# Where the operands of TensorE's matmuls lie in SBUF: one offset modulo 512 bytes for all weight buffers, another for the projections' inputs

## The chip, the cores and the metric

The kernel runs on one core of one Trainium2 chip, in one launch. The metric is the device time of one execution in microseconds (us), and lower is better. Times before come from three timed executions and from one execution that the hardware profiler recorded.

## The reference, cut to what matters

Two residual layers over 256 tokens of width 1024, all in float32. Layer 0 mixes tokens with a Griffin block (input projections, a short convolution, gates, a linear recurrence, an output projection), layer 1 with RWKV-7 time mixing. Behind each mixer stands a PEER channel mixer, which picks 16 of 16384 experts for each token and head:

```python
for i in range(DEPTH):                      # 2 layers
    m = rglru_mixer(x, ...) if i % 2 == 0 else rwkv7_time_mix(x, ...)
    x = layer_norm(ALPHA * x + m, ...)
    # PEER: scores -> top 16 of 128 x 128 -> gate = softmax(scores)
    #   act = gelu(x . u[eid]);  c = sum over the chosen (gate * act) * v[eid]
    c = peer_channel_mix(x, peer_w_q[i], peer_sub_keys[i], peer_u[i], peer_v[i])
    x = layer_norm(ALPHA * x + c, ...)
```

## The kernel before

The kernel does not gather the chosen experts. It multiplies x by all 16384 rows of u, multiplies the result by a dense matrix of gates that is zero where an expert was not chosen, and multiplies that by all rows of v. A PEER layer therefore streams 16 blocks of query weights (the first 2 of them take another path), 128 blocks of u and 128 blocks of v, each 128 x 1024 float32 (512 KB), through one class, `Stream`. The Griffin and RWKV projections go the same way.

For each block, `Stream.prep` makes two parts: `whi`, the block rounded to float32r by ScalarE (line 90), and `wlo`, the remainder, by VectorE (line 91). There are three pairs of buffers, whi0/wlo0 to whi2/wlo2, taken in turn. A product of two float32 matrices is three float32r matmuls: high by high, high by low, low by high.

Each matmul has two SBUF operands. The stationary one (128 x 128) is brought in by a weight load that runs under the matmul before it; the moving one (128 x 256 or 128 x 512) is streamed. The two big groups of matmuls differ in which operand is which:

```python
# proj (line 317), for u, the query weights, and the Griffin and RWKV inputs: weights stationary, x moving, 256 columns
for db in range(NDB):                               # 8, so 24 matmuls in a call
    s = slice(db * 128 + c0, db * 128 + c0 + n)
    for l, r in ((wh, hi), (wh, lo), (wl, hi)):
        nc.tensor.matmul(out, l[:, s], r[:, db, :], start=(k == 0), stop=(k == 23))
# rows (line 327), for v and the output projections: coefficients stationary, weights moving, 512 columns
for k, (l, r) in enumerate(((ch, wh), (ch, wl), (cl, wh))):
    for dh in dhs:                                  # 12 matmuls in a call: 2 x 3 x 2
        nc.tensor.matmul(accs[2 * tb + dh], l[:, ts], r[:, dh * 512:dh * 512 + 512], ...)
```

Slices of an operand lie a multiple of 512 bytes apart, so an operand keeps its offset modulo 512 through a whole call. These offsets, read from the built program's allocation, are:

```
tile (bytes modulo 512)                        before            after
whi0, wlo0                                     192, 192          192, 192
whi1, wlo1                                     384, 448          192, 192
whi2, wlo2                                     64, 64            192, 192
xhi, xlo: input of u, query weights, Griffin   128               128
ch, cl: coefficients of v                      128               192
xh, xl: input of Griffin's gates (line 530)    64                128
mr, mk, mv: inputs of RWKV's r, k, v           288               128
yh, yl: stationary in Griffin's output         64                192
oh, ol: stationary in RWKV's output            384               224
sl: late coefficients and weights of v         352               352
```

Below, d is the offset of the next stationary slice minus that of the operand that streams meanwhile, modulo 512. In proj of u, before, d is 64 with buffer 0, 256 and 320 with whi1 and wlo1, and 448 with buffer 2. In rows of v it is 448, 256 and 192, and 64. At the end of a PEER layer, the last four blocks of v and their coefficients both lie in the tile `sl`, where d is 0.

While proj of u runs, VectorE and ScalarE do what `_peer_side` yields between calls: the choice of the top 16 and the dense gates. How much of it stands between two calls is set by written budgets in the order of the code, not by the clock. VectorE's `wlo` of a block stands in that same queue, and the third matmul of a call waits for it.

Of the kernel before, what the change touches and what calls it, by code (L numbers as in the profile page):

```python
# [8 lines left out]
F32 = mybir.dt.float32  # L9
F32R = mybir.dt.float32r  # L10
F16 = mybir.dt.float16
# [8 lines left out]
T = 256  # L20
NDB = 8
# [15 lines left out]
class Stream:  # L37
# [1 line left out]


    RAW, SPLIT = 4, 3
    OFF = (0, 0, 192, 64, 128, 0, 64)

    def __init__(self, nc, pool):
        self.nc, self.pool = nc, pool
        self.items, self.nd, self.np, self.nu = [], 0, 0, 0
        self.raw, self.parts, self.held, self.live = {}, {}, [], 0
        self.place, self.marks = {}, set()
        self.nr = 0

    def room(self):


        for n in range(self.RAW):
            self.pool.tile([128, 1024], F32, name="wraw", bufs=self.RAW)
        for n, off in enumerate(self.OFF):
            if off:
# [74 lines left out]
class Sched:  # L132
# [15 lines left out]
    def seq(self, items, bias):  # L148

        self.lists.append(list(items))
        self.bias.append(bias)
# [64 lines left out]
class Trunk:  # L218
    def __init__(self, ctx, tc, a):
        self.ctx, self.tc, self.nc, self.a = ctx, tc, tc.nc, a  # L220
        nc = self.nc
        self.const = ctx.enter_context(tc.tile_pool(name="const", bufs=1))
        self.stage = ctx.enter_context(tc.tile_pool(name="stage", bufs=1))
        self.keep = ctx.enter_context(tc.tile_pool(name="keep", bufs=1))
        self.ps = ctx.enter_context(tc.tile_pool(name="ps", bufs=1, space=PSUM))
        self.ws = Stream(nc, self.stage)
        self.ws.room()


    def acc(self):  # L230
# [240 lines left out]
    def rglru(self, li, last=False, parts=True):  # L471
        nc = self.nc
        with self.tc.tile_pool(name="rg", bufs=1) as pool:
            col = self.rgcol
            accs = [self.acc() for _ in range(4)]
            tm = pool.tile([128, 5, NM], F32, name="rgtm")
# [89 lines left out]
            y, late = {}, []  # L566
# [2 lines left out]
                nc.vector.scalar_tensor_tensor(gb[:, m], gb[:, m], 1.0 / ALPHA, tt[:, m], op0=ALU.mult, op1=ALU.mult)  # L569

            def yh(m):
                y[m] = pool.tile([128, T], F32R, name="yh", bufs=self.LATE), pool.tile([128, T], F32R, name="yl", bufs=self.LATE)
                nc.scalar.activation(y[m][0], gb[:, m], AF.Copy)

# [3 lines left out]
            def out(m):  # L578
# [26 lines left out]
                xhi=seq(xhi, lambda m: [("xc", m)], "xhi", None, one("act", .36), 0),  # L605
                xlo=seq(xlo, lambda m: [("xhi", m)], "xlo", None, one("dve", .34), 0),
# [25 lines left out]
    def rwkv(self, li, x, last=False, parts=True):  # L632
# [9 lines left out]
        pool = ctx.enter_context(self.tc.tile_pool(name="rw", bufs=1))  # L642
# [2 lines left out]
        mp = ph1.enter_context(self.tc.tile_pool(name="rwm", bufs=1))  # L645
        cp = None
        col = self.rwcol
        one_ = pool.tile([128, 8], F32, name="one")
        W0, A0, KK, KA, RK, LG, LB = 6, 7, 8, 9, 10, 11, 12
        r, av = ([pool.tile([128, 4, T], F32, name=f"{nm}{n}") for n in range(2)] for nm in "ra")  # L650
# [534 lines left out]
    def peer(self, l, li, x, last=False, parts=True):  # L1185
# [3 lines left out]
        keys, p = None, None  # L1189
        for what, tb, dh, f in x:  # L1190
# [5 lines left out]
            if p is None:  # L1196
                self.ws.fill()
                keys, *ws = (self.ws.get(False) for _ in range(3))
                p = self.mm()
# [9 lines left out]
        with self.tc.tile_pool(name="peer", bufs=1) as pool:  # L1209
# [8 lines left out]
            def fill(us):  # L1218
                self.budget += us
                while self.budget > 0:  # L1220
                    c = next(side, None)
                    if c is None or c < 0:
                        self.budget = 0.0
                        return
                    self.budget -= c

            def finish():
                while self.g_done < T:
                    assert next(side, 0) >= 0 or self.g_done == T
# [4 lines left out]
            def scores(q):  # L1234
                for tb in range(2):
                    sp = self.aux()
                    for a in range(2):
                        nc.tensor.matmul(sp[:, a * 128:a * 128 + 128], qt[q][:, a, tb * 128:tb * 128 + 128],  # L1238
                                         keys[:, ((q - 1 + a) % 8) * 128:((q - 1 + a) % 8) * 128 + 128], start=True, stop=True)
                    nc.scalar.activation(self.sc[tb][:, q - 1:q + 1, :], sp[:, :256].rearrange("p (a n) -> p a n", a=2), AF.Copy)  # L1240
                self.q_done = q + 1

            for q in range(16):
# [3 lines left out]
                if q >= 2:  # L1247
                    if q % 2 == 0:
                        p = self.mm()
# [9 lines left out]
            def act(sp, i):  # L1259


                n, pv, sv = self.g_done, sp.rearrange("p (a t) -> p a t", a=2), two(i)
                if n < T:
                    nc.scalar.activation(sv[:, :, n:], pv[:, :, n:], AF.Gelu_apprx_tanh)  # L1264
                if n:
                    nc.scalar.activation(pv[:, :, :n], pv[:, :, :n], AF.Gelu_apprx_tanh)
                    nc.vector.tensor_tensor(sv[:, :, :n], pv[:, :, :n], sv[:, :, :n], op=ALU.mult)
                self.s_done = i + 2


            for i in range(128):
                if i % 2 == 0:
                    prev, sp = (sp if i else None), self.mm()
                self.proj(sp[:, (i % 2) * T:(i % 2) * T + T])
                if i == 0:
                    scores(15)
                    self.ws.done()
                assert self.chosen or i < 80
                if i % 2 == 0 and i:
                    act(prev, i - 2)  # L1280
                if i == 127:
                    act(sp, 126)
                fill(SFILL)
                if i == 124:
                    finish()

                    first = [pool.tile([128, T], F32R, name=f"c{n}") for n in range(2)]
                    nc.scalar.activation(first[0], S[0][:, 0, :], AF.Copy)
                    nc.vector.tensor_tensor(first[1], S[0][:, 0, :], first[0].bitcast(F32), op=ALU.subtract)

            ch = self.keep.tile([128, 4, 2, T], F32R, name="ch", tag="xhi")
            cl = self.keep.tile([128, 4, 2, T], F32R, name="cl", tag="xlo")

            def c_at(i):

                if i < 128 - self.LATE:
                    n = (i // 2) % 4
                    return ch[:, n], cl[:, n]  # L1300
                i += 9 * self.LATE - 128
                return [sl[:, n:n + 2, :] for n in (i, i + self.LATE)]
# [7 lines left out]
            for i in range(128):  # L1310
# [11 lines left out]
                c = (wh, wl, *(first if i == 0 else (t[:, i % 2] for t in c_at(i - i % 2))))  # L1322
# [27 lines left out]
    def _peer_side(self, pool, S, carve):  # L1350
# [14 lines left out]
        for hp in range(16):  # L1365
            while self.q_done <= hp:
                yield -1.0
            for tb in range(2):
                s = self.sc[tb][:, hp, :]
                t = tmp[nt % 4]  # L1370
# [22 lines left out]
        for tb in range(2):  # L1393
# [6 lines left out]
            for r in range(5):  # L1400
                n = LENS[r]
# [7 lines left out]
            for h in range(8):  # L1409
                s = cb[:, h, :]  # L1410
                t = tmp[nt % 4][:, :NCAND]
# [35 lines left out]
            p = self.aux()  # L1447
# [12 lines left out]
        def products():  # L1460


            oa, ob, b, t0 = made.pop(0)
            p = self.aux().rearrange("p (t i) -> p t i", t=4)
            for t in range(4):
                bb, j = b + t // 2, t % 2
                for q in range(2):
                    nc.tensor.matmul(p[:, t, :], oa[:, bb, :, j], ob[:, q, bb, :, j], start=(q == 0), stop=(q == 1))  # L1468
            summed.append((p, t0))

        def gmul():

            p, t0 = summed.pop(0)
            ts = slice(t0, t0 + 4)
            c = 1.0 / (GS * ALPHA)
            for n in range(2):
                m = min(max(self.s_done - 64 * n, 0), 64)
                pi = p[:, :, 64 * n:64 * n + 64].rearrange("p t i -> p i t")
                if m:
                    nc.vector.scalar_tensor_tensor(S[n][:, :m, ts], pi[:, :m], c, S[n][:, :m, ts], op0=ALU.mult, op1=ALU.mult)  # L1480
                if m < 64:
                    nc.vector.tensor_scalar(S[n][:, m:, ts], pi[:, m:], c, None, op0=ALU.mult)  # L1482
            self.g_done = t0 + 4

        for blk in range(T // 8):
            js = [pairs(jt[:, k, blk * 8:blk * 8 + 8]) for k in range(4)]
            oa = pool.tile([128, 4, 128, 2], F16, name="oa", bufs=2)
            ob = pool.tile([128, 2, 4, 128, 2], F16, name="ob", bufs=2)
            oh = pool.tile([128, 4, 128, 2], F16, name="oh")
            nc.vector.tensor_tensor(oh, num, js[0], op=ALU.is_equal)  # L1490
            nc.vector.tensor_tensor(oa, num, js[1], op=ALU.is_equal)
            yield 1.2
            for h in range(2):
                if made:
                    products()
                if len(summed) == 2:
                    gmul()
                yield 0.8
                nc.vector.tensor_tensor(ob[:, h], oh, js[2 + h], op=ALU.mult)  # L1499
                yield 0.6  # L1500
            made += [(oa, ob, 0, blk * 8), (oa, ob, 2, blk * 8 + 4)]
# [111 lines left out]
```

## Time and profile before

| | us |
|---|---|
| median of three timed runs (2082.34 to 2084.01) | 2083.37 |
| the profiled execution | 2083.83 |
| its span, first to last instruction | 2082.1 |
| TensorE busy with matmuls, share of the span | 98% |
| VectorE, ScalarE busy, share of the span | 75%, 51% |
| mean granted TensorE clock, share of full speed | 0.995 |

A busy time is the union of the intervals in which an engine worked on something. The matmuls overlap in their records, so a busy TensorE may still be slower than it could be: what counts is the time from one matmul's start to the next one's, called the pace below.

### The profile page before, as it was taken

Reading aid. Unit: us, or ns where it says so; the run is one execution under the profiler, and the core shown is the slowest. Engines: PE = TensorE matmul, PEld = TensorE weight load, DVE = VectorE, ACT = ScalarE, POOL = GpSimd, SP = SyncE. Lnnn points to the kernel's source line nnn. Section 1 sums busy time; section 2 is a strip of 40 time slices with the busy share of each in tenths; the row PEclk is TensorE's granted clock in tenths of the full one; section 3 lists DMA queues with packets and bytes.
Section 4 is the critical chain, followed back from the end, with each engine's and each line's share of the span. In section 5 each row is a group of like instructions: output and inputs, shape, how many; then the busy total and the mean of one; then the engine's idle time right before and its main releaser. Section 6 shows DMA issues by size and latency. Waiting matters only on the chain.

```text
span 2082.1 us, 36490 instructions
## 1 busy us (share of the span) xinstructions
PE 2044.7 (98%) x14512; PEld 1878.3 (90%) x14512; DVE 1555.5 (75%) x2992; ACT 1070.6 (51%) x1600; POOL 21.0 (1%) x58
## 2 busy tenths in 40 slices
PE   8999999999999999998999999999999999999998
PEld 8989999999988888887999999999999998888886
DVE  7879988999855555558778757988899975555555
ACT  6855654444454444454767654555444444444443
POOL 0000000000000000002000000000000000000000
PEclk9999999999999999998999999999999999999999
DMA  6555565555566666663510004566555556666664
GB/s 204 173 161 189 183 195 165 166 164 166 157 190 191 190 188 189 191 206 113 152 32 1 2 27 146 185 190 184 172 162 162 163 164 191 191 188 188 190 192 153
DMA packets 92189, 334.13 MB, mean 160 GB/s; under 512 B 10609, under 2 KB 10609, under 8 KB 92017
## 3 DMA queue, kind: packets, MB, share of 16 engines
q1 hardware_dynamic: 90720, 328.77, 51.1%
q10 hardware_dynamic: 1296, 3.02, 0.4%
q8 instruction: 114, 1.87, 0.4%
q14 instruction: 59, 0.48, 0.1%
HBM read 330.69 MB, written 1.05 MB: 159 GB/s over the span
## 4 chain that ended last, share of the span: by engine, by line
PE 92%; DVE 4%; ACT 2%; issue 1%; DMA 0%; SPq 0%; ACTq 0%; DVEq 0%
PE mm L317 42%; PE acc L327 36%; PE acc L911 3%; PE aux L1468 3%; DVE wlo L91 1%; PE aux L530 1%; PE mm L1203 1%; PE aux L1238 1%; PE acc L987 1%; ACT whi L90 1%; PE acc L963 1%; PE aux L758 1%; PE acc L304 0%; PE mm L936 0%; PE aux L1046 0%
## 5 line engine op out<-in xcount | busy, mean ns | idle before, releaser
L91 DVE TENSOR_TENSOR wlo<-wraw,whi 128x1024 fp32r<-128x1024 f32 x597 | 729.3, 1222 | 406.8 <-ACT whi L90 403.7
L90 ACT ACTIVATE whi<-wraw 128x1024 fp32r<-128x1024 f32 x597 | 631.7, 1059 | 742.5 <-PE mm L317 370.6
L317 PE MATMUL mm<-xhi,whi 128*128 128x256 f32 x2448 | 694.6, 284 | 0.3 <-ACT gb L558 0.3
L317 PE MATMUL mm<-xhi,wlo 128*128 128x256 f32 x2448 | 683.3, 279 | 2.3 <-DVE wlo L91 2.2
L317 PE MATMUL mm<-xlo,whi 128*128 128x256 f32 x2448 | 682.5, 279 | 0.0
L317 PEld LDWEIGHTS mm<-xhi,wlo 128*128 128x128 f32 x2448 | 462.6, 189 | 3.0 <-DVE wlo L91 2.9
L317 PEld LDWEIGHTS mm<-xhi,whi 128*128 128x128 f32 x2448 | 460.2, 188 | 0.5 <-ACT gb L558 0.5
L317 PEld LDWEIGHTS mm<-xlo,whi 128*128 128x128 f32 x2448 | 460.1, 188 | 0.0
L327 PE MATMUL acc<-whi,cl 128*128 128x512 f32 x984 | 308.0, 394 | 0.0
L327 PE MATMUL acc<-wlo,ch 128*128 128x512 f32 x984 | 307.0, 393 | 0.0
L327 PE MATMUL acc<-whi,ch 128*128 128x512 f32 x984 | 306.8, 393 | 0.0
L327 PEld LDWEIGHTS acc<-whi,ch 128*128 128x128 f32 x984 | 184.9, 188 | 43.2
L327 PEld LDWEIGHTS acc<-whi,cl 128*128 128x128 f32 x984 | 185.0, 188 | 42.3
L327 PEld LDWEIGHTS acc<-wlo,ch 128*128 128x128 f32 x984 | 184.6, 188 | 42.1
L1499 DVE TENSOR_TENSOR ob<-oh,jt 128x1024 f16<-128x1024 f16 x128 | 87.1, 680 | 0.0
L1307 DVE TENSOR_TENSOR cl<-S,ch 128x512 fp32r<-128x512 f32 x124 | 84.6, 684 | 0.0
L1468 PE MATMUL aux<-ob,oa 128*128 128x128 f16 x1024 | 80.4, 220 | 1.6 <-DVE S L1482 0.9
L1306 ACT ACTIVATE ch<-S 128x512 fp32r<-128x512 f32 x124 | 76.3, 617 | 0.0
L1480 DVE SCALAR_TENSOR_TENSOR S<-aux,S 128x256 f32<-128x256 f32 (+4 forms) x224 | 69.7, 346 | 2.7 <-PE aux L1468 2.7
L1468 PEld LDWEIGHTS <-oa 128*128 128x128 f16 x1024 | 59.1, 97 | 7.6 <-DVE S L1482 1.6
L1264 ACT ACTIVATE S<-mm 128x512 f32<-128x512 f32 (+36 forms) x118 | 53.8, 456 | 0.1
L1490 DVE TENSOR_TENSOR oh<-iota,jt 128x1024 f16<-128x1024 f16 x64 | 44.1, 688 | 1.4
(400 smaller groups left out, 2229.1 us busy)
## 6 DMA issues: line engine op xcount, KB each, us to landing
wraw<-in_u_dram SPq DMA_DIRECT2D x256, 512.0 KB, 3.5
wraw<-in_v_dram SPq DMA_DIRECT2D x256, 512.0 KB, 4.3
wraw<-in_wq_dram SPq DMA_DIRECT2D x32, 512.0 KB, 3.6
wraw<-in_wrkv_dram SPq DMA_DIRECT2D x24, 512.0 KB, 3.7
wraw<-in_win_dram SPq DMA_DIRECT2D x22, 512.0 KB, 3.8
wraw<-in_wout_dram SPq DMA_DIRECT2D x11, 512.0 KB, 3.6
wraw<-in_wax_dram SPq DMA_DIRECT2D x8, 512.0 KB, 3.5
wraw<-in_wo_dram SPq DMA_DIRECT2D x8, 512.0 KB, 3.4
```

What stands on the lines that cost most here:

```text
L90: self.nc.scalar.activation(hi, r, AF.Copy)
L91: self.nc.vector.tensor_tensor(lo, r, hi.bitcast(F32), op=ALU.subtract)
L317: nc.tensor.matmul(out, l[:, s], r[:, db, :], start=(k == 0), stop=(k == 23))
L327: nc.tensor.matmul(accs[2 * tb + dh], l[:, ts], r[:, dh * 512:dh * 512 + 512], start=False, stop=(last and k == 2), skip_group_check=True)
L911: return quadt(lambda o, u: nc.tensor.matmul(o, lhsT[:, u, :], rhs[:, u, :], start=True, stop=True))
L1264: nc.scalar.activation(sv[:, :, n:], pv[:, :, n:], AF.Gelu_apprx_tanh)
L1306: nc.scalar.activation(h, two(i), AF.Copy)
L1307: nc.vector.tensor_tensor(l, two(i), h.bitcast(F32), op=ALU.subtract)
L1468: nc.tensor.matmul(p[:, t, :], oa[:, bb, :, j], ob[:, q, bb, :, j], start=(q == 0), stop=(q == 1))
L1480: nc.vector.scalar_tensor_tensor(S[n][:, :m, ts], pi[:, :m], c, S[n][:, :m, ts], op0=ALU.mult, op1=ALU.mult)
L1490: nc.vector.tensor_tensor(oh, num, js[0], op=ALU.is_equal)
L1499: nc.vector.tensor_tensor(ob[:, h], oh, js[2 + h], op=ALU.mult)
```

## The change

All six weight buffers get one offset modulo 512 bytes, and the pad behind them puts the tiles that follow 448 bytes beyond it, which is 64 below it. `xhi` and `xlo` become 512 bytes longer than their data, so that the coefficients of v, which reuse their room, can start 64 bytes into it, at the weights' offset. Small pads put the gates' and RWKV's inputs where x lies and Griffin's output parts where the weights lie. The first two coefficients of v move into the room of a tile that is free by then. On every engine the instructions, their order, their operands' names (but for that last tile) and their shapes are those of before; only addresses differ.

```diff
-    OFF = (0, 0, 192, 64, 128, 0, 64)
+    OFF = (0, 0, 0, 0, 0, 0, 448)
...
+        for t in ("xhi", "xlo"):
+            self.keep.tile([128, NDB * T + 128], F32, name=t, tag=t)
...
+            pool.tile([128, 16], F32, name="off")      # in rglru
...
+                if not y:
+                    pool.tile([128, 16], F32, name="offy")
...
+        pool.tile([128, 88], F32, name="off")          # in rwkv
...
-                    first = [pool.tile([128, T], F32R, name=f"c{n}") for n in range(2)]
+                    first = pool.tile([128, 2, T], F32R, name="c", tag="oh")
+                    first = [first[:, n] for n in range(2)]
...
-            ch = self.keep.tile([128, 4, 2, T], F32R, name="ch", tag="xhi")
-            cl = self.keep.tile([128, 4, 2, T], F32R, name="cl", tag="xlo")
+            ch, cl = (self.keep.tile([128, NDB * T + 128], F32R, name=n, tag=t)[:, 16:16 + NDB * T]
+                      .rearrange("p (a b t) -> p a b t", a=4, b=2) for n, t in (("ch", "xhi"), ("cl", "xlo")))
...
-            oh = pool.tile([128, 4, 128, 2], F16, name="oh")
+            oh = pool.tile([128, 4, 128, 2], F16, name="oh", tag="oh")
```

## Rows read from the trace of the kernel before

**Rows 1.** The page: busy time of the engines, chain that ended last
```profile
PE 2044.7 (98%) x14512; PEld 1878.3 (90%) x14512; DVE 1555.5 (75%) x2992; ACT 1070.6 (51%) x1600; POOL 21.0 (1%) x58
...
PE 92%; DVE 4%; ACT 2%; issue 1%; DMA 0%; SPq 0%; ACTq 0%; DVEq 0%
PE mm L317 42%; PE acc L327 36%; PE acc L911 3%; PE aux L1468 3%; DVE wlo L91 1%; PE aux L530 1%; PE mm L1203 1%; PE aux L1238 1%; PE acc L987 1%; ACT whi L90 1%; PE acc L963 1%; PE aux L758 1%; PE acc L304 0%; PE mm L936 0%; PE aux L1046 0%
```

**Rows 2.** Windows by stage: stretch, length, busy of PE to POOL, clock, DMA share, GB/s
```profile
140.00:583.00 443.00, 441.55 (x4016) 437.75 (x4015) 394.91 (x955) 212.85 (x288) 0.00 (x0) 1.00 0.56 174
583.00:940.00 357.00, 356.97 (x1558) 290.49 (x1558) 201.20 (x207) 172.75 (x200) 0.00 (x0) 1.00 0.63 192
940.00:1276.00 336.00, 319.19 (x2445) 301.22 (x2444) 247.99 (x454) 203.78 (x452) 16.30 (x16) 0.97 0.18 57
```

**Rows 3.** TensorE's timeline, u of layer 0: first matmuls of calls; start, length
```profile
208.01 0.28 PE L317 MATMUL mm<-xhi,whi 128*128 128x256 f32 x1
...
210.73 0.28 PE L317 MATMUL mm<-xhi,whi 128*128 128x256 f32 x1
...
213.56 0.28 PE L317 MATMUL mm<-xhi,whi 128*128 128x256 f32 x1
...
216.38 0.28 PE L317 MATMUL mm<-xhi,whi 128*128 128x256 f32 x1
```

**Rows 4.** TensorE's timeline, v of layer 0: first two matmuls of four calls
```profile
670.93 0.62 PE L327 MATMUL acc<-whi,ch 128*128 128x512 f32 x2
...
673.68 0.63 PE L327 MATMUL acc<-whi,ch 128*128 128x512 f32 x2
...
676.46 0.62 PE L327 MATMUL acc<-whi,ch 128*128 128x512 f32 x2
...
679.25 0.62 PE L327 MATMUL acc<-whi,ch 128*128 128x512 f32 x2
```

**Rows 5.** TensorE's timeline, end of v, both operands in sl: three overlapping windows
```profile
928.85 9.73 PE L327 MATMUL acc<-sl 128*128 128x512 f32 x42
...
931.17 3.34 PE L327 MATMUL acc<-sl 128*128 128x512 f32 x14
...
934.11 4.47 PE L327 MATMUL acc<-sl 128*128 128x512 f32 x19
```

**Rows 6.** VectorE's timeline, u of layer 0: two low parts, the second after a wait
```profile
188.99 1.23 DVE L91 TENSOR_TENSOR wlo<-wraw,whi 128x1024 fp32r<-128x1024 f32 x1
...
243.22 1.23 DVE L91 TENSOR_TENSOR wlo<-wraw,whi 128x1024 fp32r<-128x1024 f32 x1 [2.14 <-ACT whi L90]
```

**Rows 7.** TensorE's timeline: the first matmuls that use these two low parts
```profile
194.21 0.28 PE L317 MATMUL mm<-xhi,wlo 128*128 128x256 f32 x1
...
244.34 0.28 PE L317 MATMUL mm<-xlo,whi 128*128 128x256 f32 x1
244.50 0.39 PE L317 MATMUL mm<-xhi,wlo 128*128 128x256 f32 x1
```

**Rows 8.** TensorE's timeline: Griffin's gates 14 matmuls apart, RWKV's k two calls apart
```profile
47.01 0.28 PE L530 MATMUL aux<-xl,whi 128*128 128x256 f32 x1
...
48.69 0.28 PE L530 MATMUL aux<-xh,whi 128*128 128x256 f32 x1
...
1005.07 0.28 PE L317 MATMUL mm<-mkh,whi 128*128 128x256 f32 x1
...
1010.75 0.28 PE L317 MATMUL mm<-mkh,whi 128*128 128x256 f32 x1
```

**Rows 9.** Waits: DVE of 181:259 and 400:560, ACT of 583:940; total, times, longest
```profile
DVE wlo L91 <- ACT whi L90: 4.1, 4, 2.1
...
DVE wlo L91 <- ACT whi L90: 8.5, 18, 0.8
...
ACT whi L90 <- PE acc L327: 172.8, 119, 1.7
```

**Rows 10.** Window over the rest of Griffin's block, columns as in rows 2
```profile
75.00:118.00 43.00, 42.51 (x288) 38.44 (x289) 41.26 (x72) 38.82 (x78) 0.00 (x0) 1.00 0.60 180
```

## The prediction

> **What bounds the kernel now.** I began with the page. TensorE is busy 98% of the span and 92% of the chain that ended last is TensorE's own work, most of it in two lines: proj with 42% and rows with 36% [rows 1]. The windows by stage then show that TensorE hardly waits where these two run: 441.55 of 443 us in the query and u stage, 356.97 of 357 in v, at a granted clock of 1.00, which is the upper of its two levels [rows 2]. Nothing is to be had there by removing waits. So I looked at the pace of the matmuls themselves, call by call in the timeline, and this is what the reader should see:
>
> - u, first matmuls of successive calls [rows 3]: buffer 0 takes 208.01 to 210.73, 2.72 us; buffer 1 takes 2.83; buffer 2 takes 2.82. Each call has the same 24 matmuls of 256 columns and none waits, so the pace is 113.3 ns with buffer 0 and 117.7 with the others. The pattern repeats with a period of three calls through both layers. x lies at 128 in all three; only the weights' offset differs. The pace of 113.3 belongs to d = 64, that of 117.7 to 256, 320 and 448.
> - v [rows 4]: three calls take 2.75, 2.78 and 2.79 us, together 8.32 for 36 matmuls of 512 columns, 231.1 ns each. Again the length goes by the buffer and by nothing else.
> - the end of v, where d is 0 [rows 5]: one run of 42 matmuls. The windows begin at 928.85, 931.17 and 934.11. The last holds 19 matmuls, the middle one 14, of which the last is the first of the next, so 13 lie between 931.17 and 934.11, and 10 between 928.85 and 931.17. The first 10 go at 232 ns, the next 13 at 226.2. A run outlasts its last start by 3.34 - 2.94 = 0.40 us, so the last 18 steps take 4.07 us, 226.1 ns each. With the rows' rounding the settled pace is 226 to 227; I take 226.5. It stays to the end.
>
> So the trace holds the geometry of the change already. After it, every proj of x has d = 64, as buffer 0 has now, at the same two offsets; every rows of v has d = 0, as in sl.
>
> **The change part by part.**
>
> *Query weights and u.* 14 + 128 calls in each of two layers, 284. Three calls take 8.37 us now (208.01 to 216.38) and 3 x 2.72 = 8.16 after, 0.070 us less for each call: 284 x 0.070 = 19.9 us.
>
> Of this VectorE takes some back. It must make a low part for every call, beside the choice of the experts. At 188.99 + 1.23 = 190.22 a low part is ready 3.99 us ahead of its use at 194.21; at 243.22 + 1.23 = 244.45 only 0.05 us ahead of 244.50, where the step from the matmul before is 0.16 instead of 0.11 [rows 6, 7]. The waits of VectorE between 181 and 259 us are four and come to 4.1 us [rows 9]; the longest, 2.14, stands right before 243.22 and is for ScalarE, which first had to work off what VectorE gave it late. Until there VectorE runs without a stop, so a faster TensorE meets it with its reserve used up. Of the 18 calls between the two places the change speeds up the 12 on buffers 1 and 2, 18 x 0.070 = 1.3 us in all, and nothing is left of it at 244.50. The same order of code stands in layer 1. I take back 2 x 1.3 = 2.6 us, and do not expect more: between 400 and 560 us VectorE still waits 8.5 us [rows 9], while some 50 calls there gain 3.5. **17.3 us stay.**
>
> *v.* 2 x 123 calls run with the weight buffers and the coefficients ch, cl: 2952 matmuls, at 231.1 now and 226.5 after: 13.6 us, less 2 x 10 matmuls of settling at 5.5 ns, 0.1. Nothing takes it back: ScalarE waits for TensorE to free a buffer 119 times in this stage, 172.8 us in all [rows 9], and DMA is at 0.63 [rows 2]. 512 KB in 12 x 226.5 = 2.72 us is what a call on buffer 0 in u already asks for. **13.5 us.** Bounds: the settled pace for all of it, 13.6, and the unsettled 232, a loss of 2952 x 0.9 = 2.7. I take the settled one, since nothing interrupts v between its first and last call.
>
> *Griffin.* 22 projections of x (0.070 each, 1.5 us) and 186 matmuls of gates. These go at 1.68 / 14 = 120.0 ns now [rows 8] and get d = 64: 186 x 6.7 = 1.2 us. But from 75 to 118 us VectorE is busy 41.26 of 43 us and ScalarE 38.82 [rows 10]; what is gained there is lost to them, what is gained before shifts them too. Of 0 to 2.7 I take 1.5. The 84 matmuls of Griffin's output with the weight buffers and the 48 of RWKV's are too few to matter: 5 ns on each of 132 is 0.7 us, either way.
>
> *RWKV.* 26 projections, 624 matmuls, at 5.68 / 48 = 118.3 ns [rows 8]; with d = 64 that is 5 ns less each, 3.1 us. TensorE is busy 319 of 336 us in this stage, with a chain of small steps through three engines [rows 2]; of 0 to 3.1 I take 1.5.
>
> *Everything else* is at no cost because nothing moves: the same instructions stand in the same order on every engine. The pads cost room only. The first coefficients of v move into a tile whose last reader is work of VectorE that stands ahead of them in its queue.
>
> Sum: 17.3 + 13.5 + 1.5 + 1.5 = 33.8 us. The profiled execution took 2083.83, 0.46 above the median of the three runs, so I count from it: 2083.8 - 33.8 = **2050 us**, 1.6% less.
>
> **A rule against it.** The rows say that two calls with equal work differ by 0.11 us with the buffer that they read [rows 3]. The Trainium skill, SBUF — State Buffer, section "Who interferes with whom", says that TensorE has two independent read ports, one for the moving operand and one for weight loads, and that "PE and ACT never wait on anyone"; by that, addresses would not matter and the change would give 2084 us. The trace disagrees, with 2.72 against 2.83 us.
>
> **The rivals.**
>
> A. *v does not settle.* In sl the first 10 matmuls at d = 0 ran at 232 ns, and what settled them is unknown; with ch and cl in other tiles the run could stay there. For it: that start. Against it: 31 steps in a row at 226.5 across both halves of the tokens. Time: 2083.8 - 17.3 + 2.7 - 3 = 2066.
>
> B. *VectorE becomes the bound through all of u.* For it: 394.91 of 443 us busy, and a reserve that falls to 0.05 us. Against it: the 8.5 us that it waits later, and a low part's 1.23 us in a call of 2.72. If nothing of u's gain stays: 2083.8 - 13.5 - 3 = 2067.
>
> C. *Nothing happens,* because buffer 0 is fast for another reason than d, its place in the rotation for one. Against it: within a call 23 steps read only that one buffer and are all fast. Time 2084.
>
> D. *Slower: d = 0 collides in v.* The gates' stretch of rows 8 is a call with d = 0 too (weights at 64, input at 64), and at 256 columns it is the slowest of all, 120.0 against 113.3, 5.9% more. If v's long run took that ratio, 226.5 x 1.059 = 239.9 ns, it would lose 2952 x 8.8 = 26 us against 20.3 gained elsewhere: 2089. It decides from a pace of 231.1 + 20.3 / 2.952 = 238 ns. Against it stand the rows of sl, at 512 columns.
>
> **How the numbers follow.** The forecast has 0.79, A 0.10, B 0.05, C 0.03, D 0.03. The forecast's own bounds: all of u (19.9), of v (13.6), of Griffin and RWKV (5.8) give 2044.5; without the last two items and with twice VectorE's toll, 2083.8 - 14.7 - 13.5 = 2056. Cases of one sign hold nearly all of the chance, so one range does: 2045 to 2062, which takes in the forecast and those of A and B in which part of the gain stays. Some 0.2% (4 us) is what a measurement of this kernel can tell from no change: faster 0.94 (forecast, A, B), same 0.03 (C), slower 0.03 (D).
>
> **What would show it.** In u, calls of 2.72 us whatever the buffer, and no period of three. In v, calls of 2.72 us all alike, 226.5 ns a matmul; 231 or more would be A or D. Near 240 us and again in layer 1, a wait of TensorE for wlo of about a microsecond; long waits for wlo between 400 and 560 us would be B. Gates at 113 to 114 ns. Wrong would be above all a pace in v that depends on more than d modulo 512.

## The result, and the profile after

The changed kernel takes 2058.82 us, the median of four runs (2057.97 to 2060.37), against 2083.4 us for four runs of the kernel before. The ratio is 0.9883, with a 95% interval of 0.9866 to 0.9901. The whole interval lies below 1, so the change is faster, by 24.6 us where 33.8 were forecast. In the two profiled executions the span falls from 2082.1 to 2057.8 us, 24.3, at a mean granted clock of 0.995 in both.

The page after answers to [rows 1]: the same instructions, with TensorE's busy time 26 us shorter. On the chain that ended last, TensorE's share falls from 92% to 87%, and VectorE's low parts go from 1% to 3%.

```profile
PE 2018.5 (98%) x14512; PEld 1863.1 (91%) x14512; DVE 1554.6 (76%) x2992; ACT 1069.9 (52%) x1600; POOL 21.0 (1%) x58
...
PE 87%; DVE 8%; ACT 3%; issue 1%; DMA 0%; SPq 0%; ACTq 0%; DVEq 0%
PE mm L320 37%; PE acc L330 36%; PE acc L918 3%; DVE wlo L91 3%; PE aux L1476 3%; ACT whi L90 1%; PE aux L534 1%; PE mm L1210 1%; PE aux L1245 1%; PE acc L994 1%; PE acc L970 1%; PE aux L765 1%; PE acc L307 0%; PE mm L943 0%; PE aux L1053 0%
```

The starts of each stage's first matmul, in the two traces, say where the 24.3 us came from (Griffin's row counts from the start of the span):

| stage, first matmul to first matmul | before | after | gained | forecast |
|---|---|---|---|---|
| Griffin | 144.60 | 144.09 | 0.5 | 1.5 |
| query weights and u, layer 0 | 443.14 | 439.73 | 3.4 | 8.65 |
| query weights and u, layer 1 | 443.60 | 439.46 | 4.1 | 8.65 |
| v, each layer | 340.42 | 333.90 | 6.5 | 6.75 |
| RWKV, with the end of v in `sl` | 350.51 | 347.27 | 3.2 | 1.5 |

Now v, TensorE's timeline after, the first two matmuls of four calls (start, length in us). They answer to [rows 4].

```profile
665.43 0.62 PE L330 MATMUL acc<-whi,ch 128*128 128x512 f32 x2
...
668.15 0.62 PE L330 MATMUL acc<-whi,ch 128*128 128x512 f32 x2
...
670.87 0.62 PE L330 MATMUL acc<-whi,ch 128*128 128x512 f32 x2
...
673.59 0.62 PE L330 MATMUL acc<-whi,ch 128*128 128x512 f32 x2
```

Three calls, whatever the buffer, take 2.72 us each, where [rows 4] had 2.75, 2.78 and 2.79. That is 226.7 ns a matmul, and it holds through the stage.

Next u, TensorE's timeline after, first matmuls of calls, as in [rows 3], and then two of the same stage 64 us later.

```profile
205.80 0.28 PE L320 MATMUL mm<-xhi,whi 128*128 128x256 f32 x1
...
208.52 0.28 PE L320 MATMUL mm<-xhi,whi 128*128 128x256 f32 x1
...
211.24 0.28 PE L320 MATMUL mm<-xhi,whi 128*128 128x256 f32 x1
...
213.96 0.28 PE L320 MATMUL mm<-xhi,whi 128*128 128x256 f32 x1
...
269.33 0.28 PE L320 MATMUL mm<-xhi,whi 128*128 128x256 f32 x1
...
272.16 0.28 PE L320 MATMUL mm<-xhi,whi 128*128 128x256 f32 x1
```

The first four lines are what was forecast: 2.72 us with each buffer, no period of three. The last two are not. The call between them has the same two offsets, d = 64, the same shapes, and no wait inside, and takes 2.83. The page and the mean of the group hide this. It appears when the steps of each call are set beside each other: of 142 calls in a layer's stage, 29 settle at 117.8 ns (the prediction's 117.7) in layer 0 and 24 in layer 1 (21 and 17 of them in one row), the others at 113.3. A call counts as slow here, and in all that follows, when its median step from the ninth on is over 115.5 ns.

The same view at the two ends of that slow stretch, near 254 and 315 us:

```profile
252.90 0.28 PE L320 MATMUL mm<-xlo,whi 128*128 128x256 f32 x1
...
253.92 0.28 PE L320 MATMUL mm<-xlo,whi 128*128 128x256 f32 x1
254.17 0.39 PE L320 MATMUL mm<-xhi,wlo 128*128 128x256 f32 x1
...
254.74 0.28 PE L320 MATMUL mm<-xhi,whi 128*128 128x256 f32 x1
...
256.86 0.28 PE L320 MATMUL mm<-xhi,whi 128*128 128x256 f32 x1
...
314.56 0.74 PE L1457 MATMUL aux<-ident,S 128*128 128x128 f32 x3
315.06 0.37 PE L320 MATMUL mm<-xhi,whi 128*128 128x256 f32 x1
...
315.84 0.28 PE L320 MATMUL mm<-xhi,whi 128*128 128x256 f32 x1
...
318.56 0.28 PE L320 MATMUL mm<-xhi,whi 128*128 128x256 f32 x1
```

From 252.90 to 253.92 nine steps take 1.02 us, 113.3 ns each. Then the next matmul, which needs its `wlo`, starts 0.25 us later: VectorE had this low part ready only at 252.90 + 1.22 = 254.12, as its timeline says.

```profile
252.90 1.22 DVE L91 TENSOR_TENSOR wlo<-wraw,whi 128x1024 fp32r<-128x1024 f32 x1
```

From 254.74 to 256.86 eighteen steps take 2.12 us, 117.8 ns each, inside the same call, and calls stay slow for 60 us (with one break near 266 us, to which the run `again` returns). At 314.56 three transposes come between, and from 315.84 on 24 steps take 2.72 us again.

The interruption itself is the toll that the prediction spoke of. TensorE's timeline near 242 us, with a wait that [rows 7] had as 0.16 between two starts:

```profile
242.01 0.28 PE L320 MATMUL mm<-xlo,whi 128*128 128x256 f32 x1
242.98 0.39 PE L320 MATMUL mm<-xhi,wlo 128*128 128x256 f32 x1 [0.69 <-DVE wlo L91]
```

VectorE's timeline shows the low part that it waits for, and the wait in front of it is that of [rows 6]:

```profile
241.70 1.23 DVE L91 TENSOR_TENSOR wlo<-wraw,whi 128x1024 fp32r<-128x1024 f32 x1 [2.14 <-ACT whi L90]
```

The smaller stages: TensorE's timeline, Griffin's gates 14 matmuls apart and RWKV's k two calls apart, as in [rows 8].

```profile
47.01 0.28 PE L534 MATMUL aux<-xl,whi 128*128 128x256 f32 x1
...
48.65 0.28 PE L534 MATMUL aux<-xh,whi 128*128 128x256 f32 x1
...
1002.12 0.28 PE L320 MATMUL mm<-mkh,whi 128*128 128x256 f32 x1
...
1007.56 0.28 PE L320 MATMUL mm<-mkh,whi 128*128 128x256 f32 x1
```

These gates take 1.64 / 14 = 117.1 ns, near the slower of d = 64's two paces, down from 120.0. They stand in a slow stretch: the mean over the gates' 183 steps of up to 130 ns falls from 119.1 to 114.1. The two calls of RWKV's k take 5.44 / 48 = 113.3; of the 22 projections of this stage on that line, 6 are slow.

### The profile page after: what moved, and what is told of

Read it like the earlier page. It is cut to its first block, busy times and chain, and to the rows that moved or that the text cites. A ratio compares the mean times of both kernels' runs of the same rounds, so it can differ in the third digit from the quotient of the medians.

```text
span 2057.8 us, 36490 instructions
## 1 busy us (share of the span) xinstructions
PE 2018.5 (98%) x14512; PEld 1863.1 (91%) x14512; DVE 1554.6 (76%) x2992; ACT 1069.9 (52%) x1600; POOL 21.0 (1%) x58
## 4 chain that ended last, share of the span: by engine, by line
PE 87%; DVE 8%; ACT 3%; issue 1%; DMA 0%; SPq 0%; ACTq 0%; DVEq 0%
PE mm L320 37%; PE acc L330 36%; PE acc L918 3%; DVE wlo L91 3%; PE aux L1476 3%; ACT whi L90 1%; PE aux L534 1%; PE mm L1210 1%; PE aux L1245 1%; PE acc L994 1%; PE acc L970 1%; PE aux L765 1%; PE acc L307 0%; PE mm L943 0%; PE aux L1053 0%
## 5 line engine op out<-in xcount | busy, mean ns | idle before, releaser
L330 PE MATMUL acc<-whi,cl 128*128 128x512 f32 x984 | 303.0, 389 | 0.0
L330 PE MATMUL acc<-wlo,ch 128*128 128x512 f32 x984 | 302.8, 389 | 0.0
```

## The experiments

The theory after the result: at d = 64, 256-column matmuls have two paces, 113.3 and 117.8 ns. An interruption decides which, and it holds until the next one. Rival theories for the missing 9 us: the work of VectorE and ScalarE beside u slows the matmuls; VectorE's waits alone cost it; or the pace depends on more than d. No kernel below changes what is computed; the three with interruptions add matmuls or transposes whose result nobody reads. The first four ran beside ten runs of the kernel before on the same chip (median 2084.3).

**u_only: the coefficients of v back at x's offset,** so only v's d is as it was at best before (448).

```diff
-            ch, cl = (self.keep.tile([128, NDB * T + 128], F32R, name=n, tag=t)[:, 16:16 + NDB * T]
+            ch, cl = (self.keep.tile([128, NDB * T + 128], F32R, name=n, tag=t)[:, 0:NDB * T]
```

> The change with the coefficients of v back at x's offset, so that only the projections have the new geometry (d = 64) and v runs at d = 448 on every buffer. Theory 1 (pace goes by d, and a run of proj at d = 64 has two paces that hold, 113.3 and 117.7 ns, which one depending on how it was restarted): v takes 2.75 us a call, as buffer 0 did before the change, 0.031 us x 246 = 7.6 us more than the changed kernel, about 2066.5; u as in the changed kernel, calls of 2.72 and stretches of 2.83 mixed. Rival (the slow stretches of u come from what the other engines do there): the same sum.

Measured: 2064.76 us, ratio 0.9905 (0.989 to 0.992), 1.7 below the expected 2066.5. TensorE's timeline of it, u calls where the change was slow, and v:

```profile
267.02 0.28 PE L320 MATMUL mm<-xhi,whi 128*128 128x256 f32 x1
...
269.74 0.28 PE L320 MATMUL mm<-xhi,whi 128*128 128x256 f32 x1
...
680.00 0.62 PE L330 MATMUL acc<-whi,ch 128*128 128x512 f32 x2
...
682.75 0.62 PE L330 MATMUL acc<-whi,ch 128*128 128x512 f32 x2
```

Every v call takes 2.75 us here, 228.9 ns a matmul: a v stage is 337.15 us, 3.25 longer than in the change (3.8 had been expected), with nothing else changed in it. In u the long slow stretch of layer 0 is absent (9 slow calls, 2.72 us at 267), though u runs the same instructions on the same addresses as in the change. So the program does not fix where the pace is slow.

**v_only: x alone moved to d = 448,** the rest as in the change.

```diff
-    OFF = (0, 0, 0, 0, 0, 0, 448)
+    OFF = (0, 0, 0, 0, 0, 0, 64)
...
+        self.keep.tile([128, 96], F32, name="back")    # behind xhi, xlo
...
-  ... name=n, tag=t)[:, 16:16 + NDB * T]
+  ... name=n, tag=t)[:, 112:112 + NDB * T]
```

> The change with x alone at 64 bytes beyond the weights (d = 448 in u and the query weights on every buffer) and everything else where the change has it, v at d = 0. Theory 1: v keeps 2.72 us a call; every uninterrupted call of u takes 2.83 us, also those that were on buffer 0 before, with no stretch at 2.72; u loses all it gained against before (7 us) and the third that was fast before (94 calls x 0.10 = 9.9), less some 3 us of VectorE's toll that goes with the faster pace: about 2073. Rival: if d mattered only in v, u would stay as in the changed kernel, 2059.

Measured: 2077.32 us, ratio 0.9969 (0.9957 to 0.9981): the gain in v (226.7 ns) stays, and u loses. TensorE's timeline of it, first matmuls 24 apart:

```profile
208.31 0.28 PE L321 MATMUL mm<-xhi,whi 128*128 128x256 f32 x1
...
211.13 0.28 PE L321 MATMUL mm<-xhi,whi 128*128 128x256 f32 x1
```

133 of 142 u calls are slow in layer 0 and 141 in layer 1, and the u stages are 4.0 and 4.1 us longer than in the kernel before: d = 448 in every call is worse than the mixture before, where buffer 0 was nearly always fast and buffer 2, at 448, in 23 of 94 calls. The expected time was some 4 us too low. Of the 17.6 us between the traces of the change and of this run, u has 15.7, where 13.9 had been expected, and Griffin, whose projections read the same x and which had been left out, 1.7. No matmul of u waits for `wlo` here, and u is at 117.8 all the same: a wait is not needed for the slow pace.

**shift: every tile of this part 96 bytes further,** so that all d stay and all offsets change.

```diff
-    OFF = (0, 0, 0, 0, 0, 0, 448)
+    OFF = (96, 0, 0, 0, 0, 0, 448)
```

> The change with all weight buffers and everything behind them moved on by 96 bytes: all d stay, every offset of a matmul's operand in u and v differs. Theory 1: the same time within 1.5 us of the changed kernel, 2057 to 2061, v at 2.72 us a call, u at 2.72 with some stretches at 2.83. Rival (the offset itself counts, not the difference): other paces in u and v, by up to the 8 ns a matmul seen between buffers before, some 10 to 20 us.

Measured: 2061.45 us, ratio 0.9886 (0.9871 to 0.9901), the change's within its interval, though 0.45 above the expected range. v is again at 226.7 ns. Slow u calls: 47 and 35, in layer 0 from the stage's start to 267 us, where the change has them from 254 to 314, and in layer 1 at 1347 to 1362 and 1368 to 1437 us, where the change has 1387 to 1435. So d matters and not the offset itself, as far as one shift can show, and the slow stretches move.

**spread: the choice of the experts gets a smaller budget for each u call,** so it lasts three calls longer and VectorE's reserve is not used up.

```diff
-                fill(SFILL)                                  # SFILL = 1.7
+                fill(SFILL if self.chosen else 1.6)
```

> The changed kernel with a budget of 1.6 instead of 1.7 for the side work between two calls of u until the experts are chosen, so that VectorE has less to do for each call there and more calls to do it in. Theory 1: the waits of TensorE for wlo between 220 and 260 us and in layer 1 (1.9 us a layer) shrink or go, and with them the restarts after which the slow pace held from 253 to 315 us and from 1387 to 1435 us (36 calls x 0.1 us): up to 7 us, 2052 to 2056, and these stretches run at 2.72 us a call. Rival (the choice of the experts on the other engines slows proj in these stretches): the slow stretch stays and moves along with that work; only the waits go, 2055 to 2057.

Measured: 2052.07 us (2050.43 to 2054.28), ratio 0.9844 (0.983 to 0.9857): faster than both kernels, and the best version here. TensorE's waits in the query and u stage of layer 0 (total, times, longest), of spread:

```profile
PE mm L320 <- ACT S L1271: 0.6, 1, 0.6
PE aux L1476 <- DVE S L1490: 0.2, 1, 0.2
PE aux L1457 <- DVE S L1453: 0.2, 1, 0.2
```

The same view of the change begins with a wait for `wlo`, of which spread has none:

```profile
PE mm L320 <- DVE wlo L91: 0.7, 1, 0.7
...
```

The u stages gain 7.6 and 7.1 us on the kernel before, 14.7 together, instead of 7.5. Steps of over 130 ns from one matmul of these calls to the next come to 30.4 us in both layers (32.9 in the change, 28.1 before), and the fp16 products that build the dense gates (`aux<-ob,oa`; below, the products of the gates) to 55.1 (58.2 and 57.1). Slow calls are 18 and 25, not many fewer than the change's 29 and 24. The expectation of the pace thus failed, though the time lies in its range: the slow stretches did not go with the waits, but still hold 9 calls from 246 to 272 us, behind a wait of 0.6 us for ScalarE, and 18 from 1389 to 1440. So the waits and the slower pace are two separate costs, and spread takes away the first.

**again: the changed kernel once more, as it is.**

> The changed kernel once more, unchanged. Theory 1 (which of the two paces a run of u takes is decided at a restart, by timing that differs from one execution to the next): stretches at 2.83 us lie at other places or have other lengths than 253 to 315 us and 1387 to 1435 us, and the total differs with their length, 0.1 us a call, 2056 to 2062. Rival (the work of the other engines, which the program fixes, slows these stretches): the same stretches again, within a call or two.

Measured: 2057.3 us; 11 and 18 slow calls, at other places. TensorE's timeline behind the same group of transposes, first of the change and then of this execution:

```profile
266.42 0.36 PE L320 MATMUL mm<-xhi,whi 128*128 128x256 f32 x1
266.86 0.28 PE L320 MATMUL mm<-xhi,whi 128*128 128x256 f32 x1
...
268.98 0.28 PE L320 MATMUL mm<-xhi,whi 128*128 128x256 f32 x1
```

```profile
265.79 0.37 PE L320 MATMUL mm<-xhi,whi 128*128 128x256 f32 x1
266.23 0.28 PE L320 MATMUL mm<-xhi,whi 128*128 128x256 f32 x1
...
268.27 0.28 PE L320 MATMUL mm<-xhi,whi 128*128 128x256 f32 x1
```

Both executions come to this place at the slow pace, and stop for the same instructions. In the change eighteen steps then take 2.12 us, 117.8 ns each: it stays slow. Here they take 2.04, 113.3 ns each. One program, one place, two paces. The expectation was right, in the time too.

**scan1, scan2, scan3: other offsets, a different d for each buffer.**

```diff
-    OFF = (0, 0, 0, 0, 0, 0, 448)
+    OFF = (480, 0, 64, 0, 384, 0, 32)       # scan1, coefficients' slice from 0
+    OFF = (128, 0, 32, 0, 128, 0, 160)      # scan2, slice from 16 as in the change
+    OFF = (64, 0, 256, 0, 128, 0, 0)        # scan3, slice from 16
```

> The changed kernel with three differences at once, one for each pair of weight buffers: d = 32, 96 and 480 in proj of u, and 480, 416 and 32 in rows of v (coefficients at x's offset). It measures paces; its total says little. Theory 1 (the pace is set by d and by how the run was restarted, never by the side work): each buffer has its own length of call, the same in both layers, out of 2.72 and 2.83 us in u; in v each buffer repeats one length, between 2.72 and 2.79. Whether a difference between 0 and 64 or next to 64 has the fast pace alone is open. Rival (d = 64 and 0 are special, all others alike): 2.83 us on every buffer of u and 2.75 to 2.79 on every buffer of v.

> As the other kernel of three differences, with d = 192, 224 and 352 in proj of u and 384, 352 and 224 in rows of v (coefficients 64 bytes beyond x). Theory 1: each buffer one length of call, 2.83 us in u wherever the difference is far from 64, as 256 and 320 had before the change; v between 2.75 and 2.79. A pace under 113 ns in u or under 226 in v anywhere would mean that the change has not found the best offsets.

> Three differences at once, as in the two kernels before: d = 128, 384 and 0 in proj of u, and 448, 192 and 64 in rows of v. After those two, only multiples of 64 have shown the fast pace of 113.3 ns at all: 64 mostly, 192 in 10 calls of 101, 448 in 2 to 23. Theory 1: if the step between operands matters only in such a way, 128, 384 or 0 may hold the fast pace too; v at 448 takes 2.75 us a call on its buffer, as when all buffers had it, 192 and 64 more. Rival (64 alone is a good difference for 256 columns, by chance of timing): 2.8 us and more on all three buffers of u.

Measured: 2099.01, 2096.86 and 2100.3 us, each slower than the kernel before beside it (2084.3, 2084.3, 2084.1). Pace of a matmul for each d: for u the median over its calls of the mean step from the ninth on, for v the mean from call to call:

| d | 0 | 32 | 64 | 96 | 128 | 192 | 224 | 352 | 384 | 416 | 448 | 480 |
|---|---|---|---|---|---|---|---|---|---|---|---|---|
| u, 256 columns, ns | 120.0 | 118.4 | 113.3 or 117.8 | 118.7 | 118.7 | 117.8 | 117.8 | 117.3 | 118.7 | | 117.8 | 116.7 |
| v, 512 columns, ns | 226.7 | 232.5 | 232.4 | | | 228.9 | 233.2 | 234.0 | 232.5 | 232.8 | 228.9, 229.2 | 233.5 |

(64 of u and 0 of v are the change's, 448 of u is v_only's, and 448 of v is u_only's and scan3's.) The call of scan3 with d = 0, in TensorE's timeline, matmuls 18 apart, at 2.16 / 18 = 120.0 ns:

```profile
209.61 0.28 PE L320 MATMUL mm<-xhi,whi 128*128 128x256 f32 x1
...
211.77 0.28 PE L320 MATMUL mm<-xhi,whi 128*128 128x256 f32 x1
```

The best d of v, 0, is the worst of u; the best of u, 64, costs v 5.7 ns a matmul against 0. Only with d = 64 and 448, and in 10 of 94 calls with 192, did a u call settle at 113. So the three expectations were partly wrong. u has more lengths of call than 2.72 and 2.83 us, v goes up to 12 x 234.0 ns = 2.81 where 2.79 had been the most, and d = 128, 384 and 0 never hold the fast pace: the rival of scan3, that among these d 64 alone is good for 256 columns, came true.

**restart, restart8, restart_t: interruptions put in on purpose,** ahead of u's calls 1 to 44: one fp16 matmul, eight fp16 matmuls, three float32 transposes.

```diff
+                if 0 < i < 45:                                                     # restart
+                    nc.tensor.matmul(self.aux()[:, :128], self.iota[:, :, 0], self.iota[:, :, 0], start=True, stop=True)
...
+                    for n in range(3):                                             # restart_t, p8 = self.aux()
+                        nc.tensor.transpose(p8[:, n * 128:n * 128 + 128], self.ident, self.ident)
```

> The changed kernel with one more matmul of 128 float16 columns, whose result nobody reads, ahead of each call 1 to 44 of u, so that proj is restarted at every call before the experts are chosen, where the long slow stretches lie. Theory 1 (a restart draws one of the two paces, which then holds until the next restart): no slow stretch of more than a call or two between 190 and 310 us and in layer 1, where the changed kernel had 20 calls and 17 calls in a row, and one call in ten slow at most, as where products of the gates stand between the calls. In time it costs some 0.15 us for each of 88 restarts less 0.1 us for each slow call avoided: 2064 to 2072. Rival (the choice of the experts slows proj): calls between 250 and 310 us stay slow in spite of the restarts.

> With one float16 matmul ahead of each call, every call behind it came out slow (118 ns), 202, 115, 118, 117 at its start, while calls behind a whole group of such matmuls in the products of the gates mostly start 201, 120, 116, 114 and are fast. Here eight float16 matmuls stand ahead of calls 1 to 44 of u, in the form and number of half such a group. Theory 1 as it stands now (the timing of the restart decides the pace, and the pace then holds): nearly all these calls run at 113.3 ns, and no slow stretch lies between 190 and 330 us or in layer 1; the eight matmuls cost some 0.45 us and 0.1 for the restart, 88 x 0.55 = 48 us, 2100 to 2112. Rival (any interruption of a run leaves it slow, or the choice of the experts slows proj): they are slow, as with one matmul.

> As the kernel with eight, but three float32 transposes of a constant ahead of calls 1 to 44 of u. Where the changed kernel transposes the chosen experts between two calls, the next call starts 202, 121, 116, 114 and is fast, in both layers. Theory 1: all these calls are fast but where TensorE waits for wlo, no slow stretch of more than two calls; three transposes at some 0.11 us, 0.2 of change of kind and 0.1 of restart, 88 x 0.6 = 50 us, 2100 to 2115. Rival: slow, as with one matmul.

Measured: 2071.21, 2104.63 and 2085.75 us. On restart and restart8 the expectation of the pace failed; that their times lie in the expected ranges all the same is luck, and restart_t's lies far below its own. The first added matmul stands right behind products of the scores, and the call behind it is fast. From the second on, at 195 us, calls are slow until 317 and 333 us, and layer 1 begins in the same way at 1322 and 1339. All 82 calls of each run behind the added matmuls alone are slow, and up to 333 us only behind the three transposes of the choice does a call turn fast. So an interruption does not draw the pace anew each time. The rival of VectorE's and ScalarE's work is no better: between 195 and 250 us it stands beside fast calls in the change, and beside slow ones here. TensorE's timeline of restart at that first place; nine steps before take 1.02 us, and eighteen after it 2.12:

```profile
194.36 0.28 PE L320 MATMUL mm<-xhi,wlo 128*128 128x256 f32 x1
...
195.38 0.28 PE L320 MATMUL mm<-xhi,wlo 128*128 128x256 f32 x1
195.50 0.23 PE L1282 MATMUL aux<-iota 128*128 128x128 f16 x1
195.54 0.36 PE L320 MATMUL mm<-xhi,whi 128*128 128x256 f32 x1
...
195.97 0.28 PE L320 MATMUL mm<-xhi,whi 128*128 128x256 f32 x1
...
198.09 0.28 PE L320 MATMUL mm<-xhi,whi 128*128 128x256 f32 x1
```

In restart_t slow and fast calls alternate, one by one, from 195 to 323 us, but for one pair at 270 us, where the choice's three transposes stand beside the added ones. Two neighbouring calls in its timeline:

```profile
219.95 0.49 PE L1284 MATMUL aux<-ident 128*128 128x128 f32 x3
...
220.63 0.28 PE L320 MATMUL mm<-xhi,whi 128*128 128x256 f32 x1
...
222.75 0.28 PE L320 MATMUL mm<-xhi,whi 128*128 128x256 f32 x1
...
223.11 0.49 PE L1284 MATMUL aux<-ident 128*128 128x128 f32 x3
...
223.79 0.28 PE L320 MATMUL mm<-xhi,whi 128*128 128x256 f32 x1
...
225.84 0.28 PE L320 MATMUL mm<-xhi,whi 128*128 128x256 f32 x1
```

Eighteen steps take 2.12 us in the first and 2.05 in the second. The same transposes stand ahead of both; what differs is the pace from which TensorE came to them. That an interruption sets the pace at d = 64, and that it holds until the next one, is thereby shown for the query and u stages, where no stretch of 16 or more steps of up to 130 ns changes its pace on the way, in the change and in each of these runs with d = 64. In Griffin's block it is not so clean: in the change the pace went from 113.3 to 117.8 at 32 us with no step above 120 ns.

What in an interruption decides is shown only in part. It depends on the kind: behind eight products of the gates all 100 calls of the change are fast, also the 7 that came from a slow one, and behind sixteen 7 of 14 are slow, while eight matmuls of constants in restart8 left all 82 slow. It depends on the pace before, and, by the two executions of the change, on something finer that the trace doesn't resolve.

## Why the prediction was right, and where its sum was off

The mechanism was right: the pace goes by d modulo 512, and shift shows that it goes by d and not by the offset. What it left out is that in u, at d = 64, the pace also depends on the last interruption. The time lies in the range, 8.8 us above the forecast of 2050.

*v, 13.5 us:* right. 13.0 us came, at 226.7 ns; 226.5 had been taken from the `sl` rows. u_only puts v's d back to 448 and loses 6.5 us in its two v stages. Half of v's gain is thus d = 0 against 448, the best d of before, the other half that no buffer has a worse one.

*Query weights and u, "284 x 0.070 = 19.9 us", less 2.6:* this is the term that was mis-sized. 7.5 us came. By steps, both layers together:

- Steps of up to 130 ns, within calls and from one call to the next, fell from 760.3 to 747.1 us. Of these 13.2, 1.7 belong to 15 steps that grew longer than 130 ns and count below, so the pace gained 11.5, where 19.9 stood. First, 19.9 took the three calls of [rows 3] for all: in the whole trace 176 of 284 calls were slow before, which at 24 x 4.4 ns = 0.105 us each is 18.5. Second, d = 64 does not fix 113.3 ns: 53 calls are still slow, 5.6 us. The last 1.4 is what interruptions cost beside: some 23 of a call's 24 steps are of up to 130 ns, and the second to fourth step of a fast call take 117.2, 115.3 and 114.7 ns on average. The trace of before held the warning: 9 of its 94 calls on buffer 0 were slow.
- VectorE's toll was near the 2.6 taken back for it. Long steps went from 138 to 153 and from 28.1 to 32.9 us; without the 1.7 that the 15 added ones would have taken anyway, that is 3.1 of waiting. Another 1.1 came in the products of the gates (57.1 to 58.2), which I had put at nothing. The place was right, near 242 us and again in layer 1. I had counted 1.3 us at one place in each layer; there are several in each. spread, which moves VectorE's work, gets back 2.5 us of the long steps and 3.1 in the products, of which 0.6 goes to steps into and out of them.

*Griffin, 1.5:* 0.5 came, though the paces did what was expected: steps of up to 130 ns gained 0.9 us in the gates (119.1 to 114.1 ns on average) and 1.2 in the projections. Steps over 130 ns in the projections took 1.0 of it back, and the rest of the block 0.6. That waiting would take a part had been foreseen, but it took more.

*RWKV, 1.5:* 3.2 came, and part of that was luck. 0.3 came in the end of v, which the stage in the table takes in, and 1.7 between the first and the last of the 22 projections, which went from 118.8 to 114.8 ns a step with 6 still slow. The other 1.2 came before them and goes with the clock, which was at its lower level there for part of the time in both traces: eight transposes took 1.55 us before and 1.19 after, at a granted clock of 0.50 and 0.64 around them, and the last 22 steps of the two projections that stand apart 220.8 ns each before and 184.2 after, at 0.51 and 0.61. The bound of 3.1 counted 26 projections; the trace has 24.

The rivals. A: v settled at once and stayed. B: VectorE takes part of u's gain, and not all; it waits 7.3 us between 400 and 560 us, as against 8.5 in [rows 9]. C: a time of 2084 is excluded by the ratio's interval, and buffers 1 and 2 are as fast as buffer 0 once they have its d. The Trainium skill, SBUF — State Buffer, section "Who interferes with whom", lets TensorE's two read ports work without waiting on anyone. The runs disagree: u_only and the change differ in the start of the coefficients alone, and in 3.25 us for each v stage. D: d = 0 is the best of v's d and the worst of u's. Its premise holds (120.0 ns in scan3), and it does not carry over to 512 columns.

Open: what sets the pace at an interruption, and why d = 64 suits 256 columns and d = 0 suits 512.

## What to carry to other kernels

When TensorE is busy all the time, compare the pace of equal calls over a whole stage: a difference that goes by the buffer is an address, and the relative offset of stationary and moving operand modulo 512 bytes is worth a scan, for each shape of matmul apart. Before multiplying a gain seen in three calls by the number of calls, count how many calls show it, and how many of the good ones don't. When the engine that bounds gets faster, look for the neighbour whose reserve is smallest; here a budget changed from 1.7 to 1.6 brought 0.4% more.

## What was unexpected of the hardware

- At d = 64, float32r matmuls of 256 columns run at 113.3 or 117.8 ns on the same addresses, and in the change kept to one of them for 17 calls (48 us) without a break.
- A wait of 0.25 us turned the fast pace into the slow one, and one of 0.97 us did not; one fp16 matmul on constants left all 82 calls behind it slow, eight products of the gates left 100 of 100 fast; three float32 transposes turned slow into fast and fast into slow.
- At d = 0 the pace is the best for 512 columns (226.7 ns, against up to 234.0 at other d) and the worst for 256 (120.0).
